# Encoder block kernel: a fifth pair of split buffers after the mixer, and the channel mixer's first weights fetched ahead of the last residual sum

## The chip, the cores and the metric

The kernel runs on one core of one Trainium2 chip. The metric is the device time of one execution in microseconds (us), given as the median of several runs. Five engines work beside each other and meet at semaphores: TensorE (PE, with its weight loads shown apart as PEld), VectorE (DVE), ScalarE (ACT), GpSimd (POOL) and SyncE (SP), which issues the loads of the weights.

## The reference, cut to what matters

One residual block over 256 tokens of width 2048, all in float32:

```
u  = rms_norm(x, g_mix)
h  = x + mixer(u)                 # two gated branches, merged @ w_out (2048 x 2048)
u2 = rms_norm(h, g_ffn)
gate, up = split(u2 @ w_ffn_in)   # 2048 x 11264
h  = h + (silu(gate) * up) @ w_ffn_out
out = rms_norm(h, g_final)
```

The mixer holds a sparse attention with an indexer, a state-space scan, and two sigmoid gates `u @ w_gate`. The sum `h = x + mixer(u)` is the last thing of the mixer stage, and the channel mixer (`w_ffn_in`, `w_ffn_out`) multiplies with it.

## The kernel before, in words

Weights stream from memory in raw blocks of 4 x 512 columns (1 MB) into three raw buffers (pool `wraw`). Every float32 operand of a product is split into two parts: `hi` is a copy rounded by ACT, `lo` is the raw value minus `hi`, made by DVE. Each product then takes three matmuls (hi by hi, lo by hi, hi by lo). A half block (1024 columns a partition, 2 tiles of depth) takes one `hi` and one `lo` buffer; there are four of each (pools `whi`, `wlo`), used in turn, so a split of a later half can start only when PE has finished with the half four before it.

In the stages with plain products, `gemm` (L143) loads a block, splits its halves and issues the matmuls into PSUM. `w_o` (the output product of the mixer) runs in four column blocks `nb` (L716 on). After each, the residual sum on DVE writes `h` (L723), ACT squares it for the norm (L724), and `quad_ops` (L667) makes the operands of the channel mixer for this quarter ("quad") of the depth: PE transposes (L678), ACT copies (L681), DVE sums and differences (L684 to L691), and splits into the tiles `opa`, `opb` and `opx`. `opb` comes from the pool `mid` of eight buffers.

The channel mixer's first product goes through `block7` (L752): blocks of 2 x 2 tiles are multiplied with seven products in place of eight, for three of the four quads. For that, the first weight block of such a quad needs sums of weights: `ta` (L780, 1024 columns) and the two halves of `tb` (L781, L782), which are split like the others. `ta` and `tb` also come from the pool `mid`, and in the code they stand behind the `opb` of the last quad. Eleven calls of `pair` (L805) each run the four quads into seven PSUM tiles and take these out with a chain of DVE sums (L810) and ACT operations (L812 to L818, L822, L823); all seven PSUM banks of the pool are in use in each pair. Five pairs are followed by a `w_f2` product, then six more pairs and the second `w_f2` product, and the final norm.

The order of the instructions on each engine is written by a planner from the order of the code, with priorities: loads and splits of weights stand under `high_priority(PRE)` with PRE = 3000, the evictions of a pair under `2 * PRE` (L809). Each engine takes its instructions strictly in the planned order. `issue_after` adds an order on one engine, without a wait between engines.

Short-lived scratch of the mixer comes from the pool `sm`: rope's `rtmp`, the indexer's `qih`, `qil` and `relu`, the scan's `cbm`, and at the very end also `jk`, the squares for the final norm (L847).

Of the kernel before, what the change touches and what calls it, by code (L numbers as in the profile page):

```python
# [2 lines left out]

# [11 lines left out]
P = 128  # L15
# [47 lines left out]
def hybrid_block(ctx, tc, xt, x, consts, cols, heads, gfin, w_a, w_i, w_m, w_g, w_ab, w_sb, w_o, w_f1, w_f2, out):  # L63
# [7 lines left out]
    mid = ctx.enter_context(tc.tile_pool(name="mid", bufs=8))  # L71
    ev = ctx.enter_context(tc.tile_pool(name="ev", bufs=2))
    sm = ctx.enter_context(tc.tile_pool(name="sm", bufs=2))
    dp = ctx.enter_context(tc.tile_pool(name="dp", bufs=1, space=bass.MemoryType.DRAM))
    pctx = ctx.enter_context(ExitStack())
    mm = pctx.enter_context(tc.tile_pool(name="mm", bufs=4, space=bass.MemoryType.PSUM))
# [5 lines left out]
    def nm(s):  # L82
        uid[0] += 1
        return f"{s}_{uid[0]}"
# [40 lines left out]
    def rstd_of(ssq, n, name, eng=nc.gpsimd):  # L125
# [14 lines left out]
            eng.tensor_tensor(r, r, q, ALU.mult)  # L140
        return r

    def gemm(w, first, N, nk, lhs, before=None, late=0):  # L143


        ps = [mm.tile([P, 512], F32, tag="mm", name=nm("mm")) for _ in range(T)]
        held = []

        def one(t, kt, rh, rl):
            lh, ll = lhs(kt, t)  # L150
            o = ps[t][:, :N]
            nc.tensor.matmul(o, lh, rh, start=(kt == 0), stop=False)  # L152
            nc.tensor.matmul(o, lh, rl, start=False, stop=False)  # L153
            nc.tensor.matmul(o, ll, rh, start=False, stop=(kt == nk - 1))  # L154

        kt = 0
        for c in range(nk // 4):
            if before is not None:
                before(c)
            with tc.high_priority(PRE):  # L160
                raw = wraw.tile([P, 4, 512], F32, tag="raw", name=nm("raw"))
                rawf = raw.rearrange("p k n -> p (k n)")
                if before is None or c > 0:
                    nc.sync.dma_start(rawf[:, : 4 * N], w[first + c])
                else:
                    for q in range(2):
                        first_load = nc.sync.dma_start(rawf[:, q * N : (q + 1) * N], w[first][:, q * N : (q + 1) * N])
            if before is not None and c == 0:
                with tc.issue_after(first_load.ins):
                    before(0, 1)  # L170
                    with tc.high_priority(PRE):
                        nc.sync.dma_start(rawf[:, 2 * N : 4 * N], w[first][:, 2 * N : 4 * N])
            for h in range(2):
                src = rawf[:, 2 * h * N : 2 * (h + 1) * N]
                with tc.high_priority(PRE):
                    if nk - late <= kt < nk - 8:
                        hi, lo = mid_t([P, 1024], F32R, name="hi"), mid_t([P, 1024], F32R, name="lo")
                    else:
                        hi = whi.tile([P, 1024], F32R, tag="hi", name=nm("hi"))
                        lo = wlo.tile([P, 1024], F32R, tag="lo", name=nm("lo"))  # L180
                    step = N if before is not None and kt == 0 else 2 * N
                    for q in range(0, 2 * N, step):
                        o = slice(q, q + step)
                        hi_ops.append(nc.scalar.activation(hi[:, o], src[:, o], AF.Copy))  # L184
                        nc.vector.tensor_tensor(lo[:, o], src[:, o], hi[:, o].bitcast(F32), ALU.subtract)  # L185
                for k in range(2):
                    rh = hi[:, k * N : (k + 1) * N]
                    rl = lo[:, k * N : (k + 1) * N]
                    for t in range(T):
                        if t > 0 and kt >= nk - late:  # L190
                            held.append((t, kt, rh, rl))
                        else:
                            one(t, kt, rh, rl)
                    kt += 1
        for a in held:
            one(*a)
        return ps
# [73 lines left out]


    xsq = [big_t([P, 8, S], name="xsq") for _ in range(2)]
    part = sm.tile([P, 2, S], F32, tag="relu", name="part")
    for i in range(2):
        with tc.issue_after(hi_ops[-5 + i].ins):
            nc.scalar.activation(xsq[i], xt_sb[i], AF.Square)
# [21 lines left out]
    def rope_apply(dst, src, t, nh, half):  # L299
# [1 line left out]
        cb, sb = (0, 128) if half == 64 else (256, 320)  # L301
        ct = rope[:, cb + t * half : cb + (t + 1) * half].unsqueeze(1)
        st = rope[:, sb + t * half : sb + (t + 1) * half].unsqueeze(1)
        tmp = sm.tile([P, 512], F32, tag="rtmp", name=nm("rtmp"))
        n = nh * 2 * half
        tv = tmp[:, :n].rearrange("p (h two d) -> p h two d", two=2, d=half)
        sv = src.rearrange("p (h two d) -> p h two d", two=2, d=half)
# [73 lines left out]
    def index_pairs(tok, npair, h0):  # L381

        for pr in range(npair):
            tq = tr_t([P, S])
            for t in range(T):
                nc.tensor.transpose(tq[:, t * P : (t + 1) * P], tok[:, t, pr * P : (pr + 1) * P], ident)
            qh = sm.tile([P, S], F32R, tag="qih", name=nm("qih"))
            ql = sm.tile([P, S], F32R, tag="qil", name=nm("qil"))
            split(qh, ql, tq)
            for t in range(T):  # L390
                n = P * (t + 1)
# [2 lines left out]
                nc.tensor.matmul(dots[:, :, :n], qh[:, tt], kbd_h[:, :, :n], start=True, stop=False)  # L394
                nc.tensor.matmul(dots[:, :, :n], qh[:, tt], kbd_l[:, :, :n], start=False, stop=False)
                nc.tensor.matmul(dots[:, :, :n], ql[:, tt], kbd_h[:, :, :n], start=False, stop=True)
                rl = sm.tile([P, 2, S], F32, tag="relu", name=nm("relu"))
                nc.scalar.activation(rl[:, :, :n], dots[:, :, :n], AF.Relu)
                for hh in range(2):
                    h = h0 + 2 * pr + hh  # L400
# [55 lines left out]
    def ssm_scores(g):  # L456
# [1 line left out]
        cps = tr_t([P, 384])  # L458
        nc.tensor.matmul(cps[:, 0:S], bT[:, g, 0:P], cT[:, g, :], start=True, stop=True)
        nc.tensor.matmul(cps[:, S:384], bT[:, g, P:S], cT[:, g, P:S], start=True, stop=True)  # L460
        cbm = sm.tile([P, 384], F32, tag="cbm", name=nm("cbm"))
        nc.vector.tensor_tensor(cbm[:, 0:P], cps[:, 0:P], tri, ALU.mult)
        nc.scalar.activation(cbm[:, P:S], cps[:, P:S], AF.Copy)
        nc.vector.tensor_tensor(cbm[:, S:384], cps[:, S:384], tri, ALU.mult)
# [50 lines left out]
    def ssm_z(g, ps, y):  # L515
# [15 lines left out]
                k = 2 * h + c  # L531
                split(yh[:, k, :], yl[:, k, :], y[:, k, :], ccol(C_GS, 4 * g + k))
        nc.scalar.activation(y, y, AF.Square)
        part = sm.tile([P, 512], F32, tag="rtmp", name=nm("ysq"))[:, :S]
        nc.vector.tensor_reduce(part, y.rearrange("p k s -> p s k"), AX.X, ALU.add)
        sqp = sd_t([P, T], name="sqp")
        for t in range(T):
# [107 lines left out]
            nc.vector.tensor_tensor(a, a, sg[:, t, :], ALU.mult)  # L645


    sga = []
    for nb in range(4):
        ps = gemm(w_g, 4 * nb, 512, KT, lhs_u)  # L650
# [17 lines left out]
    def quad_ops(q):  # L668
# [38 lines left out]

        return get


    lhs_m = lhs_quads(mT)
    h_sb = [big_t([P, D], name="h") for _ in range(T)]
# [3 lines left out]
    for nb in range(4):  # L716
        xr = ev_t([P, T, 512], "xr")
        for t in range(T):
            nc.gpsimd.dma_start(xr[:, t, :], x[t * P : (t + 1) * P, nb * 512 : (nb + 1) * 512])
        ps = gemm(w_o, 4 * nb, 512, KT, lhs_m)  # L720
        for t in range(T):
            a = h_sb[t][:, nb * 512 : (nb + 1) * 512]
            nc.vector.tensor_tensor(a, ps[t], xr[:, t, :], ALU.add)  # L723
            nc.scalar.activation(xr[:, t, :], a, AF.Square, accum_out=sq4[:, t, nb : nb + 1])  # L724
        ops.append(quad_ops(nb))
    ssq2 = sm.tile([P, T], F32, tag="ssq", name="ssq_h")
# [9 lines left out]
    sq5 = sm.tile([P, T, 5], F32, tag="sq5", bufs=1, name="sq5")  # L736
    acts = []

    def halves(raw, cuts):

        out = {}
        for i, n in cuts:
            hi = whi.tile([P, 1024], F32R, tag="hi", name=nm("hi"))[:, : n * 512]
            lo = wlo.tile([P, 1024], F32R, tag="lo", name=nm("lo"))[:, : n * 512]
            src = raw[:, i : i + n, :].rearrange("p k n -> p (k n)")
            nc.scalar.activation(hi, src, AF.Copy)  # L746
            nc.vector.tensor_tensor(lo, src, hi.bitcast(F32), ALU.subtract)  # L747
            for j in range(n):
                out[i + j] = hi[:, j * 512 : (j + 1) * 512], lo[:, j * 512 : (j + 1) * 512]
        return out  # L750

    def block7(w, first, quads, get):  # L752

# [13 lines left out]

        for q, seven in enumerate(quads):  # L770
            for part in range(2):
                with tc.high_priority(PRE):
                    raw = wraw.tile([P, 4, 512], F32, tag="raw", name=nm("raw"))
                    nc.sync.dma_start(raw.rearrange("p k n -> p (k n)"), w[first + 2 * q + part])
                    if seven and part == 0:

                        b = halves(raw, ((0, 2),))
                        ta = mid_t([P, 2, 512], name="ta")
                        tb = mid_t([P, 2, 512], name="tb")
                        nc.vector.tensor_tensor(ta, raw[:, 2:4, :], raw[:, 1:3, :], ALU.subtract)  # L780
                        nc.vector.tensor_tensor(tb[:, 0, :], raw[:, 3, :], ta[:, 0, :], ALU.subtract)  # L781
                        nc.vector.tensor_tensor(tb[:, 1, :], raw[:, 0, :], tb[:, 0, :], ALU.subtract)  # L782
                        tbs = halves(tb, ((0, 2),))
                        tas = halves(ta, ((0, 2),))
                        b.update(halves(raw, ((3, 1),)))
                    else:
                        b = halves(raw, ((0, 2), (2, 2)))
                if seven and part == 0:
                    prod(1, get(q, 0), b[1])
                    prod(2, get(q, 2), b[0])  # L790
                    prod(6, get(q, 9), tbs[0])
                    prod(4, get(q, 3), tbs[1])
                    prod(7, get(q, 1), tas[1])
                    prod(5, get(q, 8), tas[0])
                    prod(3, get(q, 12), b[3])
                else:
                    k0 = 4 if seven else 4 * part
# [5 lines left out]
        return ps  # L803

    def pair(p):  # L805
        ps = block7(w_f1, 8 * p, QUADS, lambda q, i: ops[q](i))
        xa, xb = ev_t([P, T, 512], "xa"), ev_t([P, T, 512], "xb")
        x1, x2, x3, x4 = xa[:, 0, :], xa[:, 1, :], xb[:, 0, :], xb[:, 1, :]
        r0, r1 = rstd2[:, 0:1], rstd2[:, 1:2]  # L809
# [19 lines left out]
    for p0, p1 in ((0, SPLIT_PAIRS), (SPLIT_PAIRS, NPAIR)):  # L829
# [6 lines left out]
        for nb in range(4):  # L836
# [3 lines left out]
            for t in range(T):  # L840
                n = 256 if last else 512
                for c in range(512 // n):
# [1 line left out]
                    a = h_sb[t][:, cs]  # L844
                    nc.vector.tensor_tensor(a, ps[t][:, c * n : (c + 1) * n], a, ALU.add)
                    if p0 > 0:
                        jk = sm.tile([P, 512], F32, tag="rtmp", name=nm("jk"))[:, :n]  # L847
                        nc.scalar.activation(jk, a, AF.Square, accum_out=sq5[:, t, nb + c : nb + c + 1])
                        nc.vector.tensor_tensor(hg[t][:, cs], a, gf[:, cs], ALU.mult)

# [104 lines left out]
```

## Time and profile before

| | us |
|---|---|
| runs | 1995.14, 1993.50, 1995.05; median 1995.05 |
| profiled execution, own time | 1993.74 |
| its span, first to last instruction | 1991.6 |
| PE busy | 1966.7 (99%) |
| DVE busy | 1425.1 (72%) |
| ACT busy | 1037.4 (52%) |

The span is what the profile's rows cover; 2.1 us of the execution's own time lie around it. An engine's busy time counts its instructions, not its waits. "Idle before" in a row is the time that the engine waited ahead of the instruction, and the arrow names what ended the wait. Matmuls overlap in the records: a 512-column matmul is shown as some 390 ns long, while one starts every 225 to 230 ns.

### The profile page before, as it was taken

How to read it: one execution, taken by the hardware profiler on the slowest of the kernel's cores; microseconds unless marked ns; L12 is line 12 of the kernel's file. 1: busy time of each engine (PE TensorE's matmuls, PEld its weight loads, DVE VectorE, ACT ScalarE, POOL GpSimd, SP SyncE). 2: the span in 40 equal slices, each digit the busy share in tenths (PEclk: the TensorE clock that was granted, in tenths of full speed). 3: DMA queues.
4: the chain of work that ended last, by engine and by line, in shares of the span. 5: the costliest groups of instructions: out<-in, count | busy, mean ns of one | idle time of the engine just before them, and what ended most of it. 6: DMA issues, size and time to landing. Idle time of an engine off the chain costs nothing.

```text
span 1991.6 us, 23532 instructions
## 1 busy us (share of the span) xinstructions
PE 1966.7 (99%) x9131; PEld 1626.6 (82%) x9131; DVE 1425.1 (72%) x1918; ACT 1037.4 (52%) x1249; POOL 36.2 (2%) x87
## 2 busy tenths in 40 slices
PE   9999999999999999999999999899999999999998
PEld 8898888888888888888888888688788887888886
DVE  7898867778768865566654656788875588888554
ACT  6575564555555544555554445455553355555443
POOL 0000000000000000000000000000000000000000
PEclk9999999999999999999999999999999999999999
DMA  7644554554554545444545555355465555555553
GB/s 279 224 162 177 190 190 169 200 201 168 194 209 169 179 163 204 174 169 169 191 170 193 186 199 192 141 209 190 169 225 189 198 192 189 206 194 205 198 190 127
DMA packets 54431, 375.70 MB, mean 189 GB/s; under 512 B 6304, under 2 KB 6816, under 8 KB 10672
## 3 DMA queue, kind: packets, MB, share of 16 engines
q1 hardware_dynamic: 51120, 360.86, 51.4%
q0 software_dynamic: 1968, 11.60, 1.6%
q10 hardware_dynamic: 1232, 1.75, 0.2%
q8 instruction: 71, 1.16, 0.2%
q14 instruction: 40, 0.33, 0.0%
HBM read 372.02 MB, written 2.16 MB: 188 GB/s over the span
## 4 chain that ended last, share of the span: by engine, by line
PE 91%; DVE 5%; DMA 2%; issue 1%; ACT 1%; POOL 0%; POOLq 0%; DVEq 0%; ACTq 0%
PE mm L152 23%; PE mm L153 23%; PE mm L154 23%; PE p L768 17%; DVE lo L747 2%; DMA raw<-in_w_f_dram 1%; PE yp L504 1%; DVE ta L780 1%; DVE xa L810 1%; PE tr L215 1%; DVE xb L810 1%; PE tr L418 1%; PE lg L606 1%; ACT hi L746 0%; PE tr L527 0%
## 5 line engine op out<-in xcount | busy, mean ns | idle before, releaser
L185 DVE TENSOR_TENSOR lo<-raw,hi 128x1024 fp32r<-128x1024 f32 (+2 forms) x513 | 618.3, 1208 | 396.8 <-ACT hi L184 395.2
L184 ACT ACTIVATE hi<-raw 128x1024 fp32r<-128x1024 f32 (+2 forms) x513 | 536.8, 1049 | 629.4 <-PE mm L154 557.2
L153 PE MATMUL mm<-lo,uh 128*128 128x512 f32 (+2 forms) x1184 | 461.2, 390 | 0.0
L154 PE MATMUL mm<-hi,ul 128*128 128x512 f32 (+2 forms) x1184 | 458.4, 388 | 0.0
L152 PE MATMUL mm<-hi,uh 128*128 128x512 f32 (+2 forms) x1184 | 453.3, 389 | 1.2 <-ACT hi L184 1.2
L768 PE MATMUL p<-hi,opa 128*128 128x512 f32 x924 | 307.5, 391 | 0.6 <-ACT hi L746 0.6
L152 PEld LDWEIGHTS mm<-hi,uh 128*128 128x128 f32 x1184 | 222.5, 188 | 44.6 <-ACT hi L184 2.1
L154 PEld LDWEIGHTS mm<-hi,ul 128*128 128x128 f32 x1184 | 222.8, 188 | 42.3 <-DVE ul L206 0.3
L153 PEld LDWEIGHTS mm<-lo,uh 128*128 128x128 f32 x1184 | 223.0, 188 | 40.9 <-DVE lo L185 0.3
L746 ACT ACTIVATE hi<-raw 128x1024 fp32r<-128x1024 f32 (+1 forms) x176 | 167.4, 975 | 115.4 <-PE p L768 93.6
L747 DVE TENSOR_TENSOR lo<-raw,hi 128x1024 fp32r<-128x1024 f32 (+1 forms) x176 | 193.0, 1118 | 32.9 <-ACT hi L746 32.7
L768 PEld LDWEIGHTS p<-hi,opa 128*128 128x128 f32 x924 | 173.8, 188 | 37.4 <-ACT hi L746 1.9
L768 PE MATMUL p<-lo,opa 128*128 128x512 f32 x462 | 181.8, 394 | 4.8 <-DVE lo L747 4.7
L153 PE MATMUL mm<-lo,act 128*128 128x512 f32 x352 | 137.2, 390 | 0.0
L154 PE MATMUL mm<-hi,act 128*128 128x512 f32 x352 | 137.0, 389 | 0.0
L152 PE MATMUL mm<-hi,act 128*128 128x512 f32 x352 | 136.6, 390 | 0.0
L768 PE MATMUL p<-hi,opb 128*128 128x512 f32 x352 | 127.8, 392 | 7.8 <-ACT hi L746 7.8
L768 PEld LDWEIGHTS p<-lo,opa 128*128 128x128 f32 x462 | 86.9, 188 | 26.9 <-DVE lo L747 9.5
L154 PE MATMUL mm<-hi,yl 128*128 128x512 f32 x256 | 100.4, 392 | 0.0
L153 PE MATMUL mm<-lo,yh 128*128 128x512 f32 x256 | 100.4, 392 | 0.0
L152 PE MATMUL mm<-hi,yh 128*128 128x512 f32 x256 | 100.2, 395 | 0.0
L768 PEld LDWEIGHTS p<-hi,opb 128*128 128x128 f32 x352 | 66.5, 189 | 22.0 <-ACT hi L746 8.2
(260 smaller groups left out, 2313.8 us busy)
## 6 DMA issues: line engine op xcount, KB each, us to landing
raw<-in_w_f_dram SPq DMA_DIRECT2D x132, 1024.0 KB, 4.8
raw<-in_w_m_dram SPq DMA_DIRECT2D x104, 1024.0 KB, 4.8
raw<-in_w_sb_dram SPq DMA_DIRECT2D x32, 1024.0 KB, 4.8
raw<-in_w_g_dram SPq DMA_DIRECT2D x32, 1024.0 KB, 4.8
raw<-in_w_ab_dram SPq DMA_DIRECT2D x16, 1024.0 KB, 4.8
raw<-in_w_o_dram SPq DMA_DIRECT2D x16, 1024.0 KB, 4.8
abc<-acum_d POOLq DMA_DIRECT2D x8, 1024.0 KB, 5.1
raw<-in_w_i_dram SPq DMA_DIRECT2D x8, 768.0 KB, 4.4
```

What stands on the lines that cost most here:

```text
L152: nc.tensor.matmul(o, lh, rh, start=(kt == 0), stop=False)
L153: nc.tensor.matmul(o, lh, rl, start=False, stop=False)
L154: nc.tensor.matmul(o, ll, rh, start=False, stop=(kt == nk - 1))
L184: hi_ops.append(nc.scalar.activation(hi[:, o], src[:, o], AF.Copy))
L185: nc.vector.tensor_tensor(lo[:, o], src[:, o], hi[:, o].bitcast(F32), ALU.subtract)
L215: nc.tensor.transpose(tp[:, c, t * P : (t + 1) * P], src(t, o), ident)
L418: nc.tensor.transpose(tp[:, c, t * P : (t + 1) * P], xk[:, t, o : o + P], ident)
L504: nc.tensor.matmul(yp[64 * c : 64 * c + 64, m, k * P :], xdt[:, k, h * 64 : (h + 1) * 64], E[:, hh, lo : lo + n], start=(k == 0), stop=(k ...
L746: nc.scalar.activation(hi, src, AF.Copy)
L747: nc.vector.tensor_tensor(lo, src, hi.bitcast(F32), ALU.subtract)
L768: nc.tensor.matmul(ps[i], x, y, start=start and j == 0, stop=left[i] == 0)
L810: add = lambda o, i, b: nc.vector.tensor_tensor(o, ps[i], b, ALU.add)
```

## The change

The scratch tiles `rtmp`, `qih`, `qil`, `relu` and `cbm` move from `sm` to a pool of their own, `smx`. It is closed behind the attention, ahead of the gates of that branch, and its bytes go to a pool `xtra` with one `hi`, one `lo` and one `tb`. A counter gives every fifth split this pair, so that from the gates on there are five pairs in turn. `tb` comes from `xtra` in every second fetch. `jk` takes a buffer of the pool `ev`.

The loading and splitting of a block in the channel mixer becomes a function `fetch`. For the very first block it is called ahead of the last quarter's residual sum, and the two residual sums get an order on DVE: behind the last operation that makes `tb`. The order of the splits, `tb` ahead of `ta`, and the products stay as they were.

```diff
+    def hl_tiles():
+        turn[0] += 1
+        if xtra and turn[0] % 5 == 0:
+            return xtra[0].tile([P, 1024], F32R, tag="hi", name=nm("hi")), xtra[0].tile([P, 1024], F32R, tag="lo", name=nm("lo"))
+        return whi.tile([P, 1024], F32R, tag="hi", name=nm("hi")), wlo.tile([P, 1024], F32R, tag="lo", name=nm("lo"))
...
+    smx_ctx.close()
+    xtra.append(ctx.enter_context(tc.tile_pool(name="xtra", bufs=1, reuse_waits="tile")))
     sga = []
...
+    def fetch(w, i, seven):
+
+        with tc.high_priority(PRE):
+            raw = wraw.tile([P, 4, 512], F32, tag="raw", name=nm("raw"))
+            nc.sync.dma_start(raw.rearrange("p k n -> p (k n)"), w[i])
+            if not seven:
+                return halves(raw, ((0, 2), (2, 2)))
+            b = halves(raw, ((0, 2),))
+            nts[0] += 1
+            ta = mid_t([P, 2, 512], name="ta")
+            tb = mid_t([P, 2, 512], name="tb") if nts[0] % 2 else xtra[0].tile([P, 2, 512], F32, tag="tb", name=nm("tb"))
+            nc.vector.tensor_tensor(ta, raw[:, 2:4, :], raw[:, 1:3, :], ALU.subtract)
+            nc.vector.tensor_tensor(tb[:, 0, :], raw[:, 3, :], ta[:, 0, :], ALU.subtract)
+            b["last"] = nc.vector.tensor_tensor(tb[:, 1, :], raw[:, 0, :], tb[:, 0, :], ALU.subtract)
+            for base, t in ((6, tb), (4, ta)):
+                for j, v in halves(t, ((0, 2),)).items():
+                    b[base + j] = v
+            b.update(halves(raw, ((3, 1),)))
+            return b
...
         ps = gemm(w_o, 4 * nb, 512, KT, lhs_m)
+        if nb == 3:
+            ahead = fetch(w_f1, 0, QUADS[0])
         for t in range(T):
             a = h_sb[t][:, nb * 512 : (nb + 1) * 512]
-            nc.vector.tensor_tensor(a, ps[t], xr[:, t, :], ALU.add)
+            with tc.issue_after(ahead["last"].ins) if nb == 3 else nullcontext():
+                nc.vector.tensor_tensor(a, ps[t], xr[:, t, :], ALU.add)
...
-                        jk = sm.tile([P, 512], F32, tag="rtmp", name=nm("jk"))[:, :n]
+                        jk = ev_t([P, 1024], "jk")[:, :n]
```

## Rows read from the trace of the kernel before

**Rows 1.** The page of the profile: busy time, share of the span and instructions of each engine.

```profile
PE 1966.7 (99%) x9131; PEld 1626.6 (82%) x9131; DVE 1425.1 (72%) x1918; ACT 1037.4 (52%) x1249; POOL 36.2 (2%) x87
```

**Rows 2.** The waits of TensorE in the whole span: what it waited for, us in total, times, longest.

```profile
PE p L768 <- ACT hi L746: 8.4, 2, 7.8
PE p L768 <- DVE lo L747: 4.8, 11, 0.8
```

**Rows 3.** Stretches of 50 us: length, then busy time (and instructions) of PE, PEld, DVE, ACT, POOL, the granted clock as a share of full speed, the DMA share, GB/s.

```profile
1050.00:1100.00 50.00, 50.00 (x222) 41.40 (x222) 24.37 (x22) 22.39 (x23) 0.00 (x0) 1.00 0.55 190
1250.00:1300.00 50.00, 41.87 (x180) 33.66 (x180) 36.50 (x41) 25.03 (x32) 2.09 (x6) 0.93 0.42 154
```

**Rows 4.** TensorE in order of time at the change of stage: start, us, engine, line, operation; idle before it and what ended that.

```profile
1254.82 0.39 PE L154 MATMUL mm<-hi,mT 128*128 128x512 f32 x1
...
1255.99 0.87 PE L678 MATMUL tr<-kc,h 128*128 128x128 f32 x6 [0.24 <-DVE h L723]
1256.62 0.48 PE L768 MATMUL p<-hi,opa 128*128 128x512 f32 x1
...
1257.85 0.39 PE L768 MATMUL p<-hi,opa 128*128 128x512 f32 x1
1266.02 0.80 PE L768 MATMUL p<-hi,opb 128*128 128x512 f32 x1 [7.78 <-ACT hi L746]
...
1269.46 0.39 PE L768 MATMUL p<-hi,opx 128*128 128x512 f32 x1
```

**Rows 5.** VectorE in order of time over the same place.

```profile
1245.46 1.23 DVE L185 TENSOR_TENSOR lo<-raw,hi 128x1024 fp32r<-128x1024 f32 x1 [0.50 <-ACT hi L184]
1248.18 1.23 DVE L747 TENSOR_TENSOR lo<-raw,hi 128x1024 fp32r<-128x1024 f32 x1 [1.49 <-ACT hi L746]
1254.57 1.37 DVE L723 TENSOR_TENSOR h<-mm,xr 128x512 f32<-128x512 f32 x2 [5.16 <-PE mm L154]
...
1258.18 0.69 DVE L684 TENSOR_TENSOR opf<-opf 128x512 f32<-128x512 f32 x1 [1.29 <-ACT opf L681]
...
1259.59 1.22 DVE L780 TENSOR_TENSOR ta<-raw 128x1024 f32<-128x1024 f32 x1
1260.72 1.22 DVE L203 TENSOR_TENSOR opa<-opf,opa 128x1024 fp32r<-128x1024 f32 x1
1261.86 0.68 DVE L203 TENSOR_TENSOR opb<-opf,opb 128x512 fp32r<-128x512 f32 x1
1262.46 0.68 DVE L781 TENSOR_TENSOR tb<-raw,ta 128x512 f32<-128x512 f32 x1
...
1264.20 0.68 DVE L782 TENSOR_TENSOR tb<-raw,tb 128x512 f32<-128x512 f32 x1
```

**Rows 6.** ScalarE in order of time over the same place.

```profile
1247.08 1.06 ACT L746 ACTIVATE hi<-raw 128x1024 fp32r<-128x1024 f32 x1 [1.66 <-PE mm L154]
1255.29 0.63 ACT L724 ACTIVATE xr<-h 128x512 f32<-128x512 f32 x1 [7.14 <-DVE h L723]
...
1259.14 0.61 ACT L202 ACTIVATE opb<-opf 128x512 fp32r<-128x512 f32 x1
1264.91 1.06 ACT L746 ACTIVATE hi<-tb 128x1024 fp32r<-128x1024 f32 x1 [5.16 <-DVE tb L782]
```

**Rows 7.** The loads of the channel mixer's weights: the DMA queue of SP in order of time (its first two issues in one row, then the third), and the time from issue to landing (of eleven loads).

```profile
1234.90 7.33 SPq L774 DMA_DIRECT2D raw<-in_w_f_dram  x2
1246.71 0.33 SPq L774 DMA_DIRECT2D raw<-in_w_f_dram  x1
DMA to landing us min/median/max: 4.6/4.8/5.4
```

**Rows 8.** A stretch of 2 us late in the gap and one of 3.44 us behind it, columns as in rows 3.

```profile
1264.00:1266.00 2.00, 0.00 (x0) 0.00 (x0) 0.88 (x2) 1.09 (x2) 0.00 (x0) 0.50 0.00 0
1266.02:1269.46 3.44, 3.44 (x9) 2.51 (x9) 3.44 (x4) 2.37 (x3) 0.00 (x0) 0.54 0.01 2
```

**Rows 9.** The end of a pair: the whole stretch of the second pair (columns as in rows 3), then DVE, ACT and PE in order of time from its last part into the next pair.

```profile
1314.47:1357.86 43.39, 42.99 (x192) 35.25 (x192) 37.67 (x43) 24.60 (x28) 0.00 (x0) 1.00 0.55 196
1345.49 1.06 ACT L746 ACTIVATE hi<-raw 128x1024 fp32r<-128x1024 f32 x1 [3.69 <-PE p L768]
1346.59 1.23 DVE L747 TENSOR_TENSOR lo<-raw,hi 128x1024 fp32r<-128x1024 f32 x1 [1.60 <-ACT hi L746]
1350.00 0.68 DVE L810 TENSOR_TENSOR xa<-p,xa 128x512 f32<-128x512 f32 x1
...
1356.59 1.21 DVE L747 TENSOR_TENSOR lo<-raw,hi 128x1024 fp32r<-128x1024 f32 x1
1357.86 0.50 PE L768 MATMUL p<-lo,opa 128*128 128x512 f32 x1 [0.40 <-DVE lo L747]
```

**Rows 10.** GpSimd: the same operation of the norm's inverse root in a scan stage and at the change of stage.

```profile
738.19 0.19 POOL L138 TENSOR_TENSOR rq<-rq,rv 128x2 f32<-128x2 f32 x1
1258.32 0.61 POOL L138 TENSOR_TENSOR rq<-rq,rv 128x2 f32<-128x2 f32 x1
```

**Rows 11.** By tile: operations, count, duration min/median/max in ns, first and last start: the last users of `rtmp` in the attention, the last transposes out of `xa`, and `jk`.

```profile
L317 DVE TENSOR_TENSOR qtok<-qtok,rtmp x8: 411/414/416, 809.5 to 962.8; 128x256 f32<-128x256 f32 x8
L215 PE MATMUL tr<-kc,xa x44: 270/272/272, 1317.8 to 1865.3; 128*128 128x128 f32 x44
L848 ACT ACTIVATE jk<-h x10: 400/614/616, 1885.8 to 1983.6; 128x512 f32<-128x512 f32 x6, 128x256 f32<-128x256 f32 x4
```

More of the change, by code (lines that the diff above doesn't have):

```diff
@@ L1 @@
 import math
-from contextlib import ExitStack
+from contextlib import ExitStack, nullcontext
 import concourse.bass as bass
@@ L73, in hybrid_block @@
     sm = ctx.enter_context(tc.tile_pool(name="sm", bufs=2))
+    smx_ctx = ctx.enter_context(ExitStack())
+    smx = smx_ctx.enter_context(tc.tile_pool(name="smx", bufs=2))
     dp = ctx.enter_context(tc.tile_pool(name="dp", bufs=1, space=bass.MemoryType.DRAM))
@@ L141, in rstd_of @@
         return r
+    xtra = []
+    turn = [0]
+    def hl_tiles():
[3 more added lines that the diff above has]
+        return whi.tile([P, 1024], F32R, tag="hi", name=nm("hi")), wlo.tile([P, 1024], F32R, tag="lo", name=nm("lo"))
     def gemm(w, first, N, nk, lhs, before=None, late=0):
@@ L178, in gemm @@
                     else:
-                        hi = whi.tile([P, 1024], F32R, tag="hi", name=nm("hi"))
-                        lo = wlo.tile([P, 1024], F32R, tag="lo", name=nm("lo"))
+                        hi, lo = hl_tiles()
                     step = N if before is not None and kt == 0 else 2 * N
@@ L273, in hybrid_block @@
     xsq = [big_t([P, 8, S], name="xsq") for _ in range(2)]
-    part = sm.tile([P, 2, S], F32, tag="relu", name="part")
+    part = smx.tile([P, 2, S], F32, tag="relu", name="part")
     for i in range(2):
@@ L303, in rope_apply @@
         st = rope[:, sb + t * half : sb + (t + 1) * half].unsqueeze(1)
-        tmp = sm.tile([P, 512], F32, tag="rtmp", name=nm("rtmp"))
+        tmp = smx.tile([P, 512], F32, tag="rtmp", name=nm("rtmp"))
         n = nh * 2 * half
@@ L386, in index_pairs @@
                 nc.tensor.transpose(tq[:, t * P : (t + 1) * P], tok[:, t, pr * P : (pr + 1) * P], ident)
-            qh = sm.tile([P, S], F32R, tag="qih", name=nm("qih"))
-            ql = sm.tile([P, S], F32R, tag="qil", name=nm("qil"))
+            qh = smx.tile([P, S], F32R, tag="qih", name=nm("qih"))
+            ql = smx.tile([P, S], F32R, tag="qil", name=nm("qil"))
             split(qh, ql, tq)
@@ L396, in index_pairs @@
                 nc.tensor.matmul(dots[:, :, :n], ql[:, tt], kbd_h[:, :, :n], start=False, stop=True)
-                rl = sm.tile([P, 2, S], F32, tag="relu", name=nm("relu"))
+                rl = smx.tile([P, 2, S], F32, tag="relu", name=nm("relu"))
                 nc.scalar.activation(rl[:, :, :n], dots[:, :, :n], AF.Relu)
@@ L460, in ssm_scores @@
         nc.tensor.matmul(cps[:, S:384], bT[:, g, P:S], cT[:, g, P:S], start=True, stop=True)
-        cbm = sm.tile([P, 384], F32, tag="cbm", name=nm("cbm"))
+        cbm = smx.tile([P, 384], F32, tag="cbm", name=nm("cbm"))
         nc.vector.tensor_tensor(cbm[:, 0:P], cps[:, 0:P], tri, ALU.mult)
@@ L533, in ssm_z @@
         nc.scalar.activation(y, y, AF.Square)
-        part = sm.tile([P, 512], F32, tag="rtmp", name=nm("ysq"))[:, :S]
+        part = smx.tile([P, 512], F32, tag="rtmp", name=nm("ysq"))[:, :S]
         nc.vector.tensor_reduce(part, y.rearrange("p k s -> p s k"), AX.X, ALU.add)
@@ L708, in quad_ops, with halves @@
         return get
+    def halves(raw, cuts):
+        out = {}
+        for i, n in cuts:
+            hi, lo = (v[:, : n * 512] for v in hl_tiles())
+            src = raw[:, i : i + n, :].rearrange("p k n -> p (k n)")
+            nc.scalar.activation(hi, src, AF.Copy)
+            nc.vector.tensor_tensor(lo, src, hi.bitcast(F32), ALU.subtract)
+            for j in range(n):
+                out[i + j] = hi[:, j * 512 : (j + 1) * 512], lo[:, j * 512 : (j + 1) * 512]
+        return out
+    nts = [0]
+    def fetch(w, i, seven):
[16 more added lines that the diff above has]
+            return b
     lhs_m = lhs_quads(mT)
@@ L737, in hybrid_block, with block7 @@
     acts = []
[L739 to L752, printed above, removed]
+    def block7(w, first, quads, get, ahead=None):
         n7 = sum(quads)
@@ L771, in block7 @@
             for part in range(2):
[L772 to L787, printed above, removed]
+                if q == part == 0 and ahead is not None:
+                    b = ahead
+                else:
+                    b = fetch(w, first + 2 * q + part, seven and part == 0)
                 if seven and part == 0:
@@ L790, in block7 @@
                     prod(2, get(q, 2), b[0])
[L791 to L794, printed above, removed]
+                    prod(6, get(q, 9), b[6])
+                    prod(4, get(q, 3), b[7])
+                    prod(7, get(q, 1), b[5])
+                    prod(5, get(q, 8), b[4])
                     prod(3, get(q, 12), b[3])
@@ L805, in pair @@
     def pair(p):
-        ps = block7(w_f1, 8 * p, QUADS, lambda q, i: ops[q](i))
+        ps = block7(w_f1, 8 * p, QUADS, lambda q, i: ops[q](i), ahead if p == 0 else None)
         xa, xb = ev_t([P, T, 512], "xa"), ev_t([P, T, 512], "xb")
```

## The prediction, made before the change was run

> **What bounds the kernel now.** The busy shares come first: TensorE (PE) is busy for 1966.7 of 1991.6 us [rows 1], so only its idle time and the time at a low clock can be won. PE's waits say where the idle time is: 8.4 us for ACT's `hi` at L768 in two pieces, one of them 7.8 us, and 4.8 us for DVE's `lo` in 11 small pieces [rows 2]. In stretches of 50 us, the mixer's last stages show PE busy throughout, 222 matmuls in 50 us or 0.225 us each, while the stretch from 1250 us has 41.87 us and a clock of 0.93 [rows 3]. So I read the engines there in order of time. The last matmul of `w_o` starts at 1254.82, the transposes of the last quad follow, then six matmuls of the channel mixer from 1256.62, and then nothing for 7.78 us, until 1266.02 [rows 4].
>
> PE waits there for `hi` of `tb`, that ACT for `tb` (5.16 us), and `tb` stands late in DVE's queue: `ta` starts at 1259.59, `tb` ends at 1264.8 [rows 5, 6]. The data are not the reason. The three loads were issued from 1234.90 on and need 4.6 to 5.4 us [rows 7], and the split of the same block ran at 1247.08 [rows 6]. DVE itself sat idle for 5.16 us before the residual sum [rows 5]. It is order alone: `ta` starts 0.45 us after ACT began writing the last `opb` (1259.14), which stands ahead of it in the code and shares its pool. The idle time has a second price. The granted clock is 0.50 of full speed late in the gap (1.2 GHz, the lower of its two levels) and still 0.54 over 1266.02 to 1269.46 [rows 8], where eight matmuls start in 3.44 us [rows 4]; at 0.225 each they would take 1.80. That is 1.64 us.
>
> **The moved fetch.** The load goes out as now: it is already SP's first issue for the channel mixer, and it stays the first of its kind; nothing on POOL moves. The first half's split is ahead of the sums already. What moves on DVE is `ta` and two `tb`, 1.13 + 0.60 + 0.60 = 2.33 us by start-to-start times [rows 5], then `lo` of `tb`, of `ta` and of the last quarter (1.14 + 1.14 + 0.60); on ACT three `hi` (1.06, 1.06, 0.6) [rows 6]. The cover is DVE's idle 5.16 us and ACT's 7.14 us while PE finishes `w_o`. From 1249.32 (end of the first `lo`, start plus 1.14) `tb` would be done at 1251.65, its `hi` at 1252.7, its `lo` at 1253.9, that of `ta` at 1255.0, the last at 1255.6. The sums can start at 1254.57, when PE delivers.
>
> With five pairs this chain starts earlier: `hi` at 1247.08 had waited 1.66 us for PE to give a buffer back [rows 6], and one more buffer is a half block, 12 matmuls or 2.7 us, ahead. Then the last `lo` ends near 1253 and the sums lose nothing. Without it the sums start 1.0 us late. **The added order** puts the two sums, and behind them ACT's squares, PE's transposes and PE's first products, behind `tb`; that alone ends well before 1254.57. Bounds of the delay: 0, and 2.28 us (two `lo` placed ahead of the sums). I take 0.3, near the end where the splits are done early. So 7.78 + 1.64 go and 0.3 comes.
>
> **What is late next.** PE then goes on at about 1258.1: five products of three matmuls (3.4 us) to 1261.5, the second block's 24 (5.4 us) to 1266.9, then the second quad, whose `tb` is wanted six matmuls later, at 1268.3. DVE has from the end of the sums (1255.9) to do: `opf` 0.6, the norm's copy 0.1, `lo` of `opa` and `opb` 1.73, two `lo` of the second block 2.28, the second quad's first `lo`, `ta`, two `tb` and `lo` of `tb` 1.14 + 1.13 + 1.2 + 1.14 = 4.6, in all 9.3 us: 1265.2, or 1266.5 if it waits 1.29 us for ACT's copies again [rows 5]. That is in time by 1.8 to 3.1 us, less than three `lo`. I charge 1.0 us; bounds 0 and 3.4 (three `lo` late).
>
> **The fifth pair and the other `tb`.** Before the channel mixer it finds PE busy throughout [rows 3] and gives nothing. In the pairs, PE's idle time without the long gap is 8.4 - 7.78 + 4.8 = 5.4 us. A typical loss is 0.40 us at 1357.86, behind a `lo` that followed the evictions without a break [rows 9]. But DVE is busy only 37.67 of 43.39 us in that pair; 1.60 us of the rest lie just ahead of the evictions, for a `hi` that ACT held 3.69 us until PE returned a buffer. A buffer more lets that `hi` go up to 2.7 us earlier, and DVE enters the evictions with 1.6 us done, against 0.40 wanted. Bounds on this: nothing won (the planner uses the room elsewhere) and all 5.4 won. I take 3.0, past the middle, because row and loss differ by a factor of four; the rest stays for the pieces where a load was late. The page "Perfetto Trace Analysis" of the Trainium skill (section "Optimization Strategy") calls the same gap, repeating on the engine that should be full, a sign of too few buffers; by that rule alone all 5.4 us would go, 2.4 more than in the sum (1981.6). That the gap repeats the rows show; that a buffer ends it, no run here shows yet.
>
> **Costed at nothing.** The moved pools: `rtmp`'s last use is at 963 us [rows 11] and the gates' branch that first uses `xtra` comes after it, so nothing waits for the bytes; if something did, a `hi` there has four other buffers, 10.9 us of matmuls, as cover. `jk` in `ev`: the last `xa` is read at 1865.3, `jk` starts at 1885.8 [rows 11], 20 us of room; two buffers as before.
>
> **The sum.** Won: 7.78 + 1.64 + 3.0 = 12.4; paid: 0.3 + 1.0 = 1.3. Net 11.1 us. The profiled execution, 1993.74, becomes 1982.6; its own time is 1.3 under the median 1995.05, on which I put the forecast: 1984.0. Ends of this case: 7.78 + 1.64 - 2.28 - 3.4 = 3.7 us won (1991.3) and 7.78 + 1.64 + 5.4 = 14.8 won (1980.2); its likely part is 1980.5 to 1988.
>
> **Rivals.**
>
> *A, DVE short in the first pair.* Both delays at their upper ends and 1.0 us at the boundaries: 7.78 + 1.64 - 2.28 - 3.4 + 1.0 = 4.7, 1990.3. For it: DVE is busy 87% of a pair [rows 9], and the long gap also gave it time to catch up. Against: 5.7 us idle in each pair.
>
> *B, the fetch isn't early.* The planner could still place `ta` late, as it did with the data there [rows 5, 7]; then the added order drags the sums along and only the boundaries give something: about 1992. Against: in the new code no `opb` of the last quad stands ahead of `ta`.
>
> *C, slower: evictions behind splits.* The fifth pair makes one more `hi` (1.06) and `lo` (1.14) ready when a pair ends; placed inside the serial chain of evictions (DVE sums and ACT's SiLU, 1350.00 to 1358 in rows 9), they hold the next pair's PSUM banks for 2.2 us. Nine boundaries lead into another pair: 19.8 us lost against 7.78 + 1.64 - 1.3 = 8.1 won, 2006.7. It decides from 0.9 us per boundary. For it: rows 9 show splits inside that chain already, and every bank is in use. Against: the evictions have twice the splits' priority.
>
> *D, the shared port.* At 1258.32 a GpSimd operation took 0.61 us in place of 0.19, while DVE's two-input `opf` (1258.18, 0.69) ran [rows 5, 10]. The page "SBUF — State Buffer" of the Trainium skill (section "SBUF: two separate sides") says that the two share a port pair, and that the one that starts later blocks until the other is done; by it DVE can lose too. The six GpSimd operations of the norm, 2.09 us in all [rows 3], would now fall among DVE's splits. If DVE lost all of that, 9.0 us are won: 1986.0. The rows show only GpSimd paying.
>
> **Chances.** Forecast 0.57; A 0.20; B 0.08; C 0.10; D 0.05. No change here means within 0.2%, 4.0 us, so faster is below 1991.06. The forecast and D count as faster, A as 0.13 faster and 0.07 the same, B as the same, C as 0.08 slower and 0.02 the same: faster 0.75, same 0.17, slower 0.08. The range 1980 to 1992 holds the forecast, D, A and part of B; C is left out.
>
> **What would show it.** Right: `ta` and `tb` run on DVE between 1246 and 1252 us, ahead of the sums; PE has no idle piece over 1.5 us around 1255 to 1270 and the clock stays at full speed (2.4 GHz) there; PE's waits for `lo` fall below 3 us; the channel mixer's first pair ends some 8 us earlier. Wrong: a wait of PE for DVE's `h` well over 0.24 us (the order costs), new waits for `tb` of the second quad (DVE short), or waits of PE's products for ACT's or DVE's evictions at the boundaries (rival C). A time over 1992 would refute the sum, since the idle time that it removes is the largest in the trace.

## The result and the profile after

| | before | changed |
|---|---|---|
| median of the runs, us | 1994.28 (4 runs, 1993.4 to 1995.14) | 1976.88 (4 runs, 1976.07 to 1977.8) |
| profiled execution's own time | 1993.74 | 1976.07 |
| its span | 1991.6 | 1974.1 |
| PE busy | 1966.7 | 1961.1 |

The ratio is 0.9913, with a 95% interval of 0.9896 to 0.9930: 17.4 us won where 11.1 were forecast, and below the low end of the stated range (1980). The direction was right and the size was not. Even the best end that the prediction worked out, 14.8 us, is passed.

TensorE's waits in the channel mixer (the stretch from 1240 us on; what it waited for, us in total, times, longest) stand against rows 2:

```profile
PE p L804 <- ACT opf L693: 0.8, 1, 0.8
PE p L804 <- DVE lo L729: 0.4, 1, 0.4
PE tr L690 <- DVE h L772: 0.2, 1, 0.2
```

The waits of 8.4 and 4.8 us are gone; a new one of 0.8 us has come. In stretches of 50 us (columns as in rows 3), the change of stage and a stretch inside the pairs:

```profile
1250.00:1300.00 50.00, 48.37 (x215) 39.06 (x214) 40.32 (x45) 29.16 (x37) 2.08 (x6) 1.00 0.48 172
1350.00:1400.00 50.00, 50.00 (x228) 41.35 (x227) 43.76 (x50) 28.36 (x32) 0.00 (x0) 1.00 0.58 205
```

PE is busy 48.37 us where it was 41.87, and the clock stays at full speed (1.00, 2.4 GHz) where it was 0.93. TensorE in order of time at the change of stage, against rows 4:

```profile
1254.75 0.39 PE L165 MATMUL mm<-hi,mT 128*128 128x512 f32 x1
...
1255.92 0.87 PE L690 MATMUL tr<-kc,h 128*128 128x128 f32 x6 [0.24 <-DVE h L772]
...
1257.78 0.39 PE L804 MATMUL p<-hi,opa 128*128 128x512 f32 x1
1259.01 0.50 PE L804 MATMUL p<-hi,opb 128*128 128x512 f32 x1 [0.84 <-ACT opf L693]
...
1274.25 0.50 PE L804 MATMUL p<-lo,opa 128*128 128x512 f32 x1 [0.44 <-DVE lo L729]
```

The third product now starts at 1259.01 and not at 1266.02. VectorE over the same place, against rows 5:

```profile
1240.19 1.22 DVE L747 TENSOR_TENSOR ta<-raw 128x1024 f32<-128x1024 f32 x1
...
1246.13 0.69 DVE L749 TENSOR_TENSOR tb<-raw,tb 128x512 f32<-128x512 f32 x1
...
1248.11 1.23 DVE L729 TENSOR_TENSOR lo<-tb,hi 128x1024 fp32r<-128x1024 f32 x1 [0.15 <-ACT hi L728]
1250.83 1.23 DVE L729 TENSOR_TENSOR lo<-ta,hi 128x1024 fp32r<-128x1024 f32 x1 [1.49 <-ACT hi L728]
1253.18 0.69 DVE L729 TENSOR_TENSOR lo<-raw,hi 128x512 fp32r<-128x512 f32 x1 [1.12 <-ACT hi L728]
1254.49 1.37 DVE L772 TENSOR_TENSOR h<-mm,xr 128x512 f32<-128x512 f32 x2 [0.62 <-PE mm L165]
```

All of the first block is split before the residual sum, which still waits for PE and not for its place in the queue: it starts 0.08 us earlier than before.

**Where the 17.5 us sit.** The same matmul in both traces tells how far each kernel has come. Every pair has three with `lo` and `opx`; the last of them is taken as the end of the pair from here on. These are the last in the first pair, the first in the second, the last in the last pair, and the last matmul of all; the kernel before:

```profile
1290.99 0.39 PE L768 MATMUL p<-lo,opx 128*128 128x512 f32 x1
...
1313.61 0.40 PE L768 MATMUL p<-lo,opx 128*128 128x512 f32 x1
...
1834.25 0.39 PE L768 MATMUL p<-lo,opx 128*128 128x512 f32 x1
...
1982.34 0.39 PE L154 MATMUL mm<-hi,act 128*128 128x512 f32 x1
```

and the changed one:

```profile
1283.22 0.39 PE L804 MATMUL p<-lo,opx 128*128 128x512 f32 x1
...
1304.98 0.39 PE L804 MATMUL p<-lo,opx 128*128 128x512 f32 x1
...
1816.73 0.39 PE L804 MATMUL p<-lo,opx 128*128 128x512 f32 x1
...
1964.83 0.39 PE L165 MATMUL mm<-hi,act 128*128 128x512 f32 x1
```

The lead is 7.77 us at the end of the first pair, 8.63 early in the second, 17.52 at the end of the last, 17.51 at the last matmul. So 7.8 us come from the change of stage, as worked out (8.1), and 9.7 from the pairs, for which 3.0 were taken and 5.4 called the most.

**Why the waits showed too little.** A stall of the kernel before, the two matmuls around the one at 1357.86 in rows 9:

```profile
1357.08 0.39 PE L768 MATMUL p<-hi,opa 128*128 128x512 f32 x1
...
1358.20 0.63 PE L768 MATMUL p<-hi,opa 128*128 128x512 f32 x2
```

From 1357.08 to 1357.86 are 0.78 us, and the usual step is 0.227: 0.55 are lost. The row shows 0.40, since the record of the matmul before is 0.39 us long and the idle time counts from its end. The step behind the stall, 0.34 to 1358.20, loses another 0.11. So 0.40 shown is 0.66 lost. Over the pairs of the kernel before, from the end of the first on, 13 steps are 0.29 to 0.94 us too long, together 7.6 us where the waits show 5.4; one has no wait shown at all (0.52 from 1767.00 to 1767.52). With 0.1 us or a little more in the step behind each, 9.1 of the 9.7 us are found. In the changed kernel no step in that stretch is even 0.1 us too long.

### The profile page after: what moved, and what is told of

It reads as the page before. It is cut to its first block, busy times and chain, and to the rows that moved or that the text cites. A ratio compares the mean times of both kernels' runs of the same rounds, so it can differ in the third digit from the quotient of the medians.

```text
span 1974.1 us, 23523 instructions
## 1 busy us (share of the span) xinstructions
PE 1961.1 (99%) x9131; PEld 1626.0 (82%) x9131; DVE 1424.0 (72%) x1918; ACT 1040.2 (53%) x1249; POOL 36.2 (2%) x87
```

## The experiments

Theory 1 was that the change holds two separate gains, the early sums at the change of stage and the fifth pair inside the pairs. The first four runs take it apart.

**The fetch ahead alone** (four pairs, `tb` always from `mid`):

```diff
-        if xtra and turn[0] % 5 == 0:
+        if False:
...
-            tb = mid_t([P, 2, 512], name="tb") if nts[0] % 2 else xtra[0].tile([P, 2, 512], F32, tag="tb", name=nm("tb"))
+            tb = mid_t([P, 2, 512], name="tb")
```

> The changed kernel with four pairs of split buffers and every tb in the pool mid: only the fetch ahead of the residual sum is left of the change. Theory 1 (two separate gains: the early sums close the gap at the change of stage, about 8.6 us by the progress of the products at the end of the first pair; the fifth pair ends the stalls inside the pairs, 8.9 us by the same count): 1994.3 - 8.6 = 1985.7, PE's gap under 1.5 us, and the stalls of about 0.40 us shown (0.66 from start to start) at the ends of the pairs still there. Theory 2 (one gain: DVE enters the first pair ahead and stays ahead, so the stalls go with the gap): 1977 to 1979 and no such stalls.

Measured 1985.88 us (ratio 0.9959, 0.9946 to 0.9971). The gap is closed and nearly all of the stalls in the pairs stand as before; in TensorE's waits of this kernel

```profile
PE p L804 <- DVE lo L729: 5.2, 10, 1.2
```

and in order of time, where the stall at the end of its second pair has the 0.40 us of rows 9:

```profile
1350.92 0.50 PE L804 MATMUL p<-lo,opa 128*128 128x512 f32 x1 [0.40 <-DVE lo L729]
```

The end of its first pair and that of its last:

```profile
1284.07 0.39 PE L804 MATMUL p<-lo,opx 128*128 128x512 f32 x1
...
1825.94 0.39 PE L804 MATMUL p<-lo,opx 128*128 128x512 f32 x1
```

Between them lie 541.87 us, against 543.26 in the kernel before and 533.51 in the changed one. Theory 2 is out: of what the pairs gain, the early sums bring 1.4 us at most.

**The fifth pair and the second place for `tb`, without the fetch ahead:**

```diff
-            ahead = fetch(w_f1, 0, QUADS[0])
+            ahead = None
...
-            with tc.issue_after(ahead["last"].ins) if nb == 3 else nullcontext():
+            with nullcontext():
```

> The changed kernel with the fifth pair and the second tb buffer, but the first block fetched in its old place, behind the last residual sum. Theory 1: the gap of 7.8 us and the low clock behind it are back, the stalls in the pairs are gone: 1994.3 - 8.9 = 1985.4. Theory 2: the stalls come back with the gap, 1993 to 1994.

Measured 1986.99 us (0.9964, 0.9951 to 0.9976). The long wait is back, and is the only one in the channel mixer beside 0.2 us for `h`:

```profile
PE p L804 <- ACT hi L728: 8.9, 1, 8.9
```

PE and DVE at that wait, and the ends of the first pair and the last:

```profile
1267.17 0.80 PE L804 MATMUL p<-hi,opb 128*128 128x512 f32 x1 [8.93 <-ACT hi L728]
...
1264.20 1.22 DVE L729 TENSOR_TENSOR lo<-raw,hi 128x1024 fp32r<-128x1024 f32 x1
1265.34 0.68 DVE L749 TENSOR_TENSOR tb<-raw,tb 128x512 f32<-128x512 f32 x1
...
1292.89 0.39 PE L804 MATMUL p<-lo,opx 128*128 128x512 f32 x1
...
1826.41 0.39 PE L804 MATMUL p<-lo,opx 128*128 128x512 f32 x1
```

The wait is 1.15 us longer than the 7.78 before, which is most of the 1.6 us that the forecast missed: DVE now makes a `lo` at 1264.20, where the second half of `tb` stood before (rows 5), and `tb` comes 1.14 us later. The two gains are 8.6 and 7.5 us alone, 16.1 in sum, against 17.4 together. Each of the two intervals is some 2.5 us wide to a side, so the times alone can't tell the sum from the whole; the traces, one execution of each, place the difference. From the end of the first pair to that of the last, this kernel takes 533.51 us, as the changed one does. At the end of the first pair the fetch alone leads by 6.92 us and the fifth pair alone is 1.90 behind, while both together lead by 7.77. So the pairs owe their gain to the fifth pair of buffers, and where the two help one another is the first pair: alone, the fetch ahead has a stall of 1.18 us there, and the fifth pair the longer gap.

```profile
1265.15 0.50 PE L804 MATMUL p<-lo,opa 128*128 128x512 f32 x1 [1.18 <-DVE lo L729]
```

(This line is from the run with the fetch ahead alone.)

**The fifth pair and the fetch ahead, every `tb` from `mid`** (the second hunk of the first diff alone):

> The changed kernel with every tb in the pool mid; fifth pair and early fetch stay. Theory 1 (the pair of split buffers is what ends the stalls): as the changed kernel, 1976 to 1978. Rival (the second place for tb is what lets the sums run ahead): the stalls in the pairs are back, 1984 to 1986.

Measured 1976.89 us (0.9916, 0.9902 to 0.9929): the changed kernel's time, and in its trace TensorE's waits are the changed kernel's too:

```profile
PE p L804 <- ACT opf L693: 0.8, 1, 0.8
PE p L804 <- DVE lo L729: 0.4, 1, 0.4
```

The second place for `tb` is worth nothing that can be measured; the pair of split buffers ends the stalls. How much of that is the buffer itself, and how much the new order that the planner writes on DVE with it, was not tried apart.

**Buffers of their own for the first sums, nothing moved in the code** (four pairs, no fetch ahead):

```diff
+            own = nts[0] == 1
-            ta = mid_t([P, 2, 512], name="ta")
+            ta = xtra[0].tile([P, 2, 512], F32, tag="ta", name=nm("ta")) if own else mid_t([P, 2, 512], name="ta")
```

(`tb` in the same way.)

> Four pairs, the first block fetched in its old place in the code; only the first ta and tb get buffers of their own in place of two of the pool mid. Theory 1 (ta was late because its buffer was handed out behind the last opb's, in the order of the code): the sums run ahead without being moved in the code, the gap closes, about 1985.7 as with the early fetch alone. Rival (the place in the code decides through the priority): the gap of 7.8 us stays, 1994.

Measured 1985.53 us (0.9959, 0.9947 to 0.9972). VectorE in order of time:

```profile
1239.91 1.22 DVE L748 TENSOR_TENSOR ta<-raw 128x1024 f32<-128x1024 f32 x1 [0.54 <-DMA raw<-in_w_f_dram]
...
1243.73 0.68 DVE L750 TENSOR_TENSOR tb<-raw,tb 128x512 f32<-128x512 f32 x1
```

`ta` runs at 1239.91, as soon as its load lands, with the code in its old order. So what held it until 1259.59 in the kernel before was its pool: with a buffer of its own it runs early from the same place in the code. It was not that the pool was full: in the changed kernel `mid` itself gives both sums their buffers, and they are written from 1240.19 on. What is left is the turn: in the code, `ta` takes its buffer behind the last `opb`. That buffers are handed out in that order is the reading that fits these runs; no view shows it directly. The change reaches the same by its place in the code. What the order that it adds with `issue_after` does by itself was not tried.

**Three, six pairs, and the new wait.** The next three look at the size of the stalls and at what is left. Three pairs in the kernel before:

```diff
-    whi = ctx.enter_context(tc.tile_pool(name="whi", bufs=4))
+    whi = ctx.enter_context(tc.tile_pool(name="whi", bufs=3))
```

(`wlo` in the same way.)

> The kernel before with three pairs of split buffers in place of four. Theory (the number of buffers sets how far DVE can work ahead of the evictions, and each stall costs some 0.27 us more than the idle time shown): more and longer stalls at the ends of the pairs, 2004 to 2020, and the added time equals the excess of PE's starts over a step of 0.227 us, not the idle time that the waits show. Rival (DVE's load alone sets the stalls, the buffers only move them): 1993 to 1997.

Measured 2024.55 us (1.0151, 1.0136 to 1.0167): 30.3 us lost, more than forecast. The rival is out, but so is a part of the theory's number. TensorE's waits at L768:

```profile
PE p L768 <- ACT hi L746: 9.3, 2, 7.8
PE p L768 <- DVE lo L747: 8.0, 13, 0.8
PE p L768 <- DVE xb L810: 3.9, 9, 1.0
```

They have grown by 8.0 us against rows 2. Counted from start to start behind the first pair, 100 steps are more than 0.1 us too long, 31.9 us together, where the kernel before has 28 such steps and 9.4 us. That is 22.5 us more, and the last matmul of all is 22.9 us further behind the end of the first pair. The profiled executions are 32.0 us apart (2025.76 against 1993.74); the other 9.1 lie outside that stretch: the mixer's last product ends 3.0 us later, from there to the end of the first pair it takes 2.9 longer, and behind the last matmul 3.2. So for the pairs the steps give the time and the waits a third of it.

Six pairs (`tb` in `mid`, and the warm-up operand there too, for room):

```diff
-        if xtra and turn[0] % 5 == 0:
+        if xtra and turn[0] % 6 > 3:
...
-    xtra.append(ctx.enter_context(tc.tile_pool(name="xtra", bufs=1, reuse_waits="tile")))
+    xtra.append(ctx.enter_context(tc.tile_pool(name="xtra", bufs=2, reuse_waits="tile")))
```

> Six pairs of split buffers from the gates on, tb in the pool mid, early fetch as in the changed kernel; to make room the operand of the warm-up matmuls takes a buffer of the pool mid. Theory (the stalls in the pairs were the whole gain and are gone with five): 1976 to 1977.5. Rival (each further pair goes on paying as the fifth did): 1972 or less.

Measured 1975.61 us (0.9906, 0.9889 to 0.9922), 0.4 under the forecast and far from the rival. No step in the pairs is too long, and none was left with five: from the end of the first pair to that of the last it again takes 533.51 us. The difference to five pairs is within the intervals; what the traces show, 0.4 us at the last matmul, lies in the first pair, where the stall at 1274.25 is gone and that for `opf` stays:

```profile
PE p L804 <- ACT opf L693: 0.7, 1, 0.7
```

The last run takes that stall away: ACT's squares of the last quarter go behind the copies that empty the transposes (five pairs, `tb` in `mid`).

```diff
-            nc.scalar.activation(xr[:, t, :], a, AF.Square, accum_out=sq4[:, t, nb : nb + 1])
+            if nb < 3:
+                nc.scalar.activation(xr[:, t, :], a, AF.Square, accum_out=sq4[:, t, nb : nb + 1])
         ops.append(quad_ops(nb))
+        if nb == 3:
+            for t in range(T):
+                with tc.issue_after(quad_last[0].ins):
+                    nc.scalar.activation(xr[:, t, :], h_sb[t][:, nb * 512 : (nb + 1) * 512], AF.Square, accum_out=sq4[:, t, nb : nb + 1])
```

> The changed kernel (tb in the pool mid, as in e3_pair_ahead) with ACT's two squares of the last quarter put behind the four copies that empty the transposes. Theory: the product that waits 0.84 us for those copies needs the PSUM bank that they free; the copies start 0.6 to 1.2 us earlier, and that stall (1.0 us from start to start) shrinks to under 0.3: 1976.9 - 0.8 = 1976.1, to be seen in the trace more than in the time. Rival: the product waits for something else that ends then, the stall stays and the time is 1976.9.

Measured 1975.18 us (0.9904, 0.9889 to 0.9919), the fastest of all, though its interval overlaps that of the changed kernel. ACT in order of time:

```profile
1257.07 1.57 ACT L695 ACTIVATE opf<-tr,colp 128x256 f32<-128x256 f32 x4 [0.22 <-PE tr L692]
1258.51 0.65 ACT L781 ACTIVATE xr<-h 128x512 f32<-128x512 f32 x1
```

and PE:

```profile
1258.34 0.39 PE L811 MATMUL p<-hi,opa 128*128 128x512 f32 x1
1258.69 0.50 PE L811 MATMUL p<-hi,opb 128*128 128x512 f32 x1
```

The squares now stand behind the last copy, and the third product starts 0.35 us behind the matmul before it, with no wait shown. That the wait was for ACT's copies is shown; that it was for a PSUM bank they free was not tried by itself. DVE's stall at 1274.25 is gone here as well, though nothing was meant to change it; why, no run shows. TensorE's only wait in the channel mixer is now

```profile
PE tr L692 <- DVE h L774: 0.2, 1, 0.2
```

## Why the prediction was right and wrong

- *What bounds the kernel.* Right: only PE's idle time and its low clock could be won, and the order on DVE, not the data, made the long gap. That `ta` stood behind the last `opb` because of their common pool is shown by the run with buffers of its own.
- *The moved fetch, 7.78 + 1.64 - 0.3.* Right. The sums lost nothing for want of their place, the clock never fell, and the lead at the end of the first pair is 7.8 us. Alone the fetch gave 8.6.
- *What is late next, 1.0 us.* Too low, and wrong in kind. The first stall is not for DVE but for ACT's copies (0.84 shown, 1.0 from start to start): ACT now has a `hi` of the second block and then the two squares ahead of them, 1255.22 to 1257.41. Only the second, 0.44 shown at 1274.25 (0.6 from start to start), is DVE's. With the step behind each, the two cost 1.8 us. That the lead of 7.8 us comes so near to the 8.1 worked out is in part luck: the stalls cost 0.8 more than was charged, and the order, for which 0.3 was taken, cost nothing.

```profile
1255.22 1.06 ACT L728 ACTIVATE hi<-raw 128x1024 fp32r<-128x1024 f32 x1 [2.08 <-PE mm L165]
1256.19 0.61 ACT L773 ACTIVATE xr<-h 128x512 f32<-128x512 f32 x1
...
1257.41 1.54 ACT L693 ACTIVATE opf<-tr,colp 128x256 f32<-128x256 f32 x4
```

- *The fifth pair, 3.0 us, bounds 0 and 5.4.* This is the step that failed. The mechanism was right: behind the first pair, the runs without it have the stalls and those with it have none. Both its value and its upper bound were mis-sized. The bound was taken as the idle time between records, "8.4 - 7.78 + 4.8 = 5.4 us", but a record of 0.39 us overlaps the next one's start by 0.16, and the step behind each stall is long too. From start to start the stalls were 9.1 to 9.4 us, and 9.7 went. Within the bound, halving was wrong as well: DVE had idle time to spare for all of them, and all went. With 9.7 in place of 3.0 the sum would have been 17.8.
- *The page "Perfetto Trace Analysis"* of the Trainium skill (section "Optimization Strategy") says that the same gap, repeating on the engine that should be full, can mean too few buffers. These traces agree: four pairs stall, five and six do not, and three lose 30 us more than four.
- *Costed at nothing.* Right: no wait for `xtra`'s bytes or for `jk`'s buffers in the waits of after.
- *Rivals.* A (DVE short in the first pair) came only as the 0.44 us at 1274.25, and as the 1.18 us of the run without the fifth pair. B (the fetch not early) did not come. C (evictions behind splits) did not either: no product waits for an eviction in the pairs. D: the GpSimd operation is again long, 0.60 us beside DVE's `opf` (rows 10 had 0.61):

```profile
1258.99 0.69 DVE L696 TENSOR_TENSOR opf<-opf 128x512 f32<-128x512 f32 x1 [1.29 <-ACT opf L693]
...
1259.13 0.60 POOL L140 TENSOR_TENSOR rq<-rq,rv 128x2 f32<-128x2 f32 x1
```

DVE's `opf` takes 0.69 us as in rows 5, so no loss on DVE shows. The Trainium skill's page "SBUF — State Buffer" (section "SBUF: two separate sides") lets the later of the two block. This trace agrees: GpSimd's is the later, by 0.14 us, and it alone is long.

## What to carry to other kernels

Price a stall of TensorE from start to start of its matmuls, not by the idle time between their records: here 0.40 us shown was 0.66 us lost, and stalls too short to be shown add up. Where an instruction runs late with its data there and its engine idle, look at what stands ahead of it in its buffer pool; a buffer of its own can do what moving the code does. And when an engine that feeds PE is busy 87% of a stage, one more buffer in front can be enough to ride over its peaks; here the next one brought nothing more in the pairs.

## What the runs showed that was not expected

Between four and three pairs of split buffers the loss is 30.3 us, between five and four about 9, and between six and five no more than the noise (1.3 us by the times, 0.4 by the traces). The price of a buffer falls steeply, though DVE's work is the same in all four, 1423 to 1425 us (the steps from four up with the early fetch in both: 1985.88, 1976.89, 1975.61).
